# One cadence for the modulation sums, in halves of a row, and one filling quantum a group moved to the last pair

## The chip, the cores and the metric

The kernel runs on one core of one Trainium2 chip. A core has a matrix engine (TensorE, PE in the profile, its weight loads as PEld), VectorE (DVE), ScalarE (ACT), GpSimd (POOL) and SyncE (SP), which here only issues DMAs. Each engine works through its own queue of instructions in order. The metric is the device time of one execution in microseconds (us).

## The reference

One encoder block for 256 tokens of width 2048, in float32:

```python
mod = silu(c) @ W_ada + b_ada          # six parts of 2048: shift_m, scale_m, gate_m, shift_f, scale_f, gate_f
h = rms_norm(x, norm_mix_w) * (1 + scale_m) + shift_m
proj = h @ w_in                        # mLSTM q,k,v,o,i,f | GDN qkv, z, beta, a | merge gates
y_a = (sigmoid(a_o) * rms_norm(bidirectional(mlstm)(...))) @ w_branch_a
y_b = (rms_norm(bidirectional(gated_delta)(...)) * silu(b_z)) @ w_branch_b
g_a, g_b = split(sigmoid(merge), 2)
x = x + gate_m * ((g_a * y_a + g_b * y_b) @ w_out)
hf = rms_norm(x, norm_ffn_w) * (1 + scale_f) + shift_f
x = x + gate_f * ((silu(hf @ W_gate) * (hf @ W_up)) @ w_down)
out = rms_norm(x, norm_final_w)
```

The mLSTM has 4 heads. The gated delta rule (GDN) has 16 heads and runs in both directions in chunks of 64 tokens; each chunk needs the inverse of a triangular matrix. `c` is a single row, so each part of `mod` is a product of a vector with a 2048x2048 matrix.

## The kernel before, in words

**Matrix products.** Weights come from memory as float32 tiles `raw` of 1 MB (three buffers), issued on SyncE's queue (L178, L210). Each half of a tile, 128x1024, is split into a high part `wh`, rounded on ScalarE (L182, L213), and a low part `wl`, the rest, on VectorE (L184, L215). TensorE then makes three products: high by high, low by high and high by low (L187 to L189 with 128x256 results in `fjob`, L234 to L236 with 128x512 results in `tjob`). `fjob` and `tjob` are generators. One `yield` is a quantum: half a `raw` tile, its `wh`, its `wl`, and 24 matmuls of 256 columns or 12 of 512.

**Filling.** The GDN heads are chains of small dependent steps between TensorE, VectorE and ScalarE. Between two such steps the program puts quanta of projections as filler: `fill(n)` (L269) takes n quanta from the list `fills`. Where the list or a stage is run out, what is left follows later; the number of quanta in all does not depend on where they are put.

**Stages.** The first stage (to about 131 us) makes parts 0 and 1 of `mod` and the first product; then come the first heads and, from about 300 us, four groups g of four GDN heads. A group has: `gdn_blocks(g)`, which loads the inverted 32x32 blocks from memory into `cg` on POOL's queue (L723), transposes them on VectorE (L725) and mixes them into `R` (L729, L730); and two pairs of heads, `gdn_phase2`, each a chain p1 (L761), p2 (L770), p3 (L783), p4 (L795), `pa`, `pb`, `pc` (L808, L819), `po` (L829 to L834), the norm (L857 to L868), and `px` (L841), whose result `obt` goes to memory (`ob_d`, L846). Between the groups stands the inversion for the next one (`invert`), with its own fills. At a group's start the loads of `cg` are issued, then `fill(8)` runs, and then come the transpose and `R`.

After the last pair come the first mLSTM heads (`pden` L962, `ph` L978) and the projection of the GDN result, `acc_yb`: its input is read back from `ob_d` into `o4` on POOL's queue (L1076) and split into `obh` (ScalarE, L1080) and `obl` (VectorE, L1081). The mLSTM's projection `acc_ya` and the output projection `acc_o` follow. The last group of `acc_o` ends in a chain of VectorE and ScalarE steps, `tmss` (L1213), the sum with x (L1216), squares (L1217) and roots, up to the transposes `pxn` (L1336) with which the FFN begins (gate, up, down, to 1960 us). `gt0`, the first gate projection, has its first two splits made ahead.

**Modulation rows.** The rows of parts 2 to 5 of `mod` are summed beside all this. Sixteen blocks of 128 rows make a part. `ask()` loads a 128x2048 block, 1 MB, into `ada` on SyncE's queue (L116); `add()` multiplies it on VectorE by the row `silu(c)` and sums it into one column of `mod` (L124); the last block of a part adds the bias (L127). `pump()` runs once a quantum and decides: in the pairs, in y_b, and in the FFN there is one buffer (`room`), a sum is owed every `every` quanta, and it is made when the load is more than two quanta old and the pair is not in its first three steps (`held`); the load for the next follows in the quantum after. Between the groups' pairs, during the inversion, `every` is 0. From the end of the last pair (L1121) until `drive(cores, 3)` (L1146) `every` is 0. From `acc_ya` on, parts 2 to 4 have three buffers in another pool (`sr`), `every` is 4, and in `acc_o` it is 0, with sums called by name at eight quanta and the rest (`sums(P)`) at the fifth quantum of the last group. In the FFN part 5 takes one row every 8 quanta.

**Order.** A scheduler places the instructions of each engine; those wrapped in `order()` (`keep_in_program_order`) stay as written among themselves.

Of the kernel before, what the change touches and what calls it, by code (L numbers as in the profile page):

```python
# [29 lines left out]
PK_ADAB = 0  # L30
PK_NMIX = 96
PK_NFFN = 112
# [20 lines left out]
def hybrid_block(ctx: ExitStack, tc: tile.TileContext, xr, nfr, crow, pk_d, cst_d, ada2, ada4, win0, winb, wint, wba, wbb, wo, wgu, wd, out, dbg=None):  # L53
    nc = tc.nc
    V, S, G, PE = nc.vector, nc.scalar, nc.gpsimd, nc.tensor

    def pool(stack, name, bufs=1, **kw):
        return stack.enter_context(tc.tile_pool(name=name, bufs=bufs, **kw))

    cp = pool(ctx, "cp")  # L60
    st = pool(ctx, "st")
    rows_p = pool(ctx, "rows")
# [9 lines left out]
    def order(ins, yes=True):  # L72

        return tc.keep_in_program_order(ins) if yes else ins
# [5 lines left out]
    row_c = crp.tile([P, D + 2], F32, name="crow")  # L80
    pk = cp.tile([P, PK_N], F32, name="pk")
# [13 lines left out]
    mods = cp.tile([P, 2, 2, KB], F32R, name="mods")  # L95
    epsc = cp.tile([P, 1], F32, name="epsc")
    V.memset(epsc, EPS)
    mod = cp.tile([P, 96], F32, name="mod")


    V.memset(row_c[:, D:], 1.0)
# [3 lines left out]
        order(S.activation(row_c[:, g * 512 : (g + 1) * 512], pc_, AF.Silu))  # L105


    room = [(rows_p, "ada", 1, 1)]
    asked, unasked, age = [], [], [0]

    def ask():

        pl, tag, bufs, _ = room[0]
        part, b = unasked.pop(0)
        raw = pl.tile([P, D], F32, tag=tag, bufs=bufs, name=f"ada{part}_{b}")
        order(nc.sync.dma_start(raw, ada4[part - 2, b]))  # L116
        asked.append((part, b, raw))
        age[0] = 0

    def add():  # L120

        part, b, raw = asked.pop(0)
        c = part * KB + b
        order(V.scalar_tensor_tensor(raw, raw, 1.0, row_c[:, :D], ALU.mult, ALU.mult, accum_out=mod[:, c : c + 1]))  # L124
        if b == KB - 1:
            c = slice(part * KB, part * KB + KB)
            V.tensor_tensor(mod[:, c], mod[:, c], pk[:, PK_ADAB + c.start : PK_ADAB + c.stop], ALU.add)  # L127

    def ada_parts(*parts):
        unasked.extend((part, b) for part in parts for b in range(KB))  # L130

    def raw_tile(shape, name):

# [5 lines left out]
    def settle(keep=0, only=None):  # L139

        now = [f for f in behind if only is None or f.__name__ == only]
        for f in now[: len(now) - keep]:
            behind.remove(f)
            f()

    count, every = [0], [0]
    owed, held = [0], [False]

    def sums(n=1):

        while n and (unasked or asked):
            while unasked and len(asked) < room[0][3]:
# [149 lines left out]
    heads, parts = {}, {}  # L302
# [190 lines left out]
    with ExitStack() as s0:  # L493
# [35 lines left out]
        ra, raw = loads(0)  # L529
# [18 lines left out]
        for b in range(KB):  # L548
            if b:
                ra, raw = loads(b)  # L550
# [332 lines left out]
    def drive(gen, n=2):  # L883
        for _ in gen:
            fill(n)
# [140 lines left out]
    for g in range(4):  # L1026
        blocks = gdn_blocks(g)
        next(blocks)
        fill(8)
        next(blocks)  # L1030
        fill(1)
        pairs = [gdn_phase2(g, p) for p in range(2)]
        if g == 3:
            settle()
            sf.close()
            mq["pool"] = pool(sq_, "mq", side="right")
            first2 = [mlstm(h) for h in range(2)]
            for c in first2:
                next(c)
        every[0] = 1  # L1040
        for p in range(2):
            pieces = stream(4 * g + 2 * p + 4)
            for n in range(1, 10):

                held[0] = n < 4
                if p == 0:
                    next(blocks, None)
                next(pairs[p], None)
                if g == 3 and n == (8, 4)[p]:
                    next(first2[p])  # L1050
                for _ in range(last[n] if g == 3 else second[n] if p else after[n]):
                    next(pieces)
            for _ in pairs[p]:
                pass

            if g < 3:
                while 4 * g + 2 * p + 5 not in heads:
                    next(pieces)
        if g < 3:
            fills.insert(0, z_job(g + 1))  # L1060
            every[0] = owed[0] = 0
            invert(g + 1)
# [93 lines left out]
    gm = room[0][0].tile([P, D], F32, name="gm")  # L1156
    dgs = {}

    def row_diag(part, g, rp):
        ms = mods[:, part == 5]  # L1160
        if not g:
            m = mod[:, part * KB : (part + 1) * KB]
            V.tensor_copy(ms[:, 0], m)
            V.tensor_tensor(ms[:, 1], m, ms[:, 0].bitcast(F32), ALU.subtract)
        dg = dgs[part, g] = rp.tile([P, 2, 4, P], F32R, tag="dg", bufs=2, name=f"dg{part}_{g}")
        for i in range(2):
            V.tensor_tensor(
                dg[:, i], ident.unsqueeze(1).broadcast_to([P, 4, P]),
                ms[:, i, 4 * g : 4 * g + 4].bitcast(F32).unsqueeze(2).broadcast_to([P, 4, P]), ALU.mult,
            )  # L1170
# [6 lines left out]
            PE.matmul(pr, onesr, woven(dg[:, i]), start=i == 0, stop=i == 1)  # L1177
        S.activation(woven(dst[:, g * 512 : (g + 1) * 512]), pr.rearrange("p (c h) -> p c h", h=2), AF.Copy)

    every[0] = 4  # L1180
    for g in range(4):
        for i, _ in enumerate(y_a(g)):
            if g and i == 3:
                merged(g - 1, mgh, mgl)
            if i in (1, 5) and g < 2:
                row_diag(2, 2 * g + i // 4, room[0][0])
# [72 lines left out]
    affn = xp.tile([P, KB], F32, name="affn")  # L1259
# [45 lines left out]
    for g in range(4):  # L1305
        if g == 3:
            root()
        for i, _ in enumerate(o_job(g, front_o if g == 3 else None) if g else o_first, 0 if g else 2):
            if i in ((4, 7), (2, 5), (2, 5), (0, 2))[g]:
                sums()  # L1310
            if g == 3 and i == 4:
                sums(P)
                V.scalar_tensor_tensor(
                    affn, mod[:, 4 * KB : 5 * KB], 1.0, pk[:, PK_NFFN : PK_NFFN + KB], ALU.add, ALU.mult
                )
    if dbg is not None and "x1" in dbg:
        G.dma_start(dbg["x1"], x1)
    room[0] = (rows_p, "ada", 1, 1)
    ada_parts(5)
    sw.close()  # L1320
    sr_.close()
# [9 lines left out]
    def block(b):  # L1331

        px = gps(f"pxn{b}")
        for t in range(2):
            f = b % 4 * P
            order(PE.transpose(px[:, t * P : (t + 1) * P], xns[b // 4][:, t, f : f + P], ident))  # L1336
        hfs[b] = hp.tile([P, T], F32, tag="hf", bufs=2, name=f"hf{b}")
        f, m = affn[:, b : b + 1], mod[:, 3 * KB + b : 3 * KB + b + 1]
# [12 lines left out]

        return scaled, high
# [89 lines left out]
    for g in range(4):  # L1442
        c = slice(g * 512, (g + 1) * 512)
# [119 lines left out]
```

## Time and profile before

| what | us |
|---|---|
| median of 3 runs | 1972.22 |
| lowest, highest | 1970.23, 1975.39 |
| profiled execution, its own time | 1972.89 |
| its span | 1970.8 |
| mean granted TensorE clock | 0.993 of full |

The span is the time from the first to the last instruction; the profiled execution's own time is 2.1 us longer. A line of a group gives line, engine, operation, output<-input, shape and count, then busy time, mean time of one in ns, and the idle time of the engine before it. A line of the timeline gives start, duration, engine, line and operation; in brackets the idle time before it and who ended it. A line of waits gives who waited for whom: total, how many times, longest. A line of a DMA issue ends in KB and the median time from issue to landing in us.

### The profile page before, as it was taken

How to read it: one execution, taken by the hardware profiler on the slowest of the kernel's cores; microseconds unless marked ns; L12 is line 12 of the kernel's file. 1: busy time of each engine (PE TensorE's matmuls, PEld its weight loads, DVE VectorE, ACT ScalarE, POOL GpSimd, SP SyncE). 2: the span in 40 equal slices, each digit the busy share in tenths (PEclk: the TensorE clock that was granted, in tenths of full speed). 3: DMA queues.
4: the chain of work that ended last, by engine and by line, in shares of the span. 5: the costliest groups of instructions: out<-in, count | busy, mean ns of one | idle time of the engine just before them, and what ended most of it. 6: DMA issues, size and time to landing. Idle time of an engine off the chain costs nothing.

```text
span 1970.8 us, 27090 instructions
## 1 busy us (share of the span) xinstructions
PE 1929.8 (98%) x10418; PEld 1705.2 (87%) x10418; DVE 1405.4 (71%) x2067; ACT 1025.8 (52%) x1551; POOL 116.6 (6%) x211
## 2 busy tenths in 40 slices
PE   8999999999999999999999999999999999999998
PEld 6878889998999899889787888788888888888886
DVE  6779886887788788866577878866665665555554
ACT  3137646765776577565534444644444444444444
POOL 0001210111011101110100000200000000000000
PEclk9999999999999999999899999999999999999999
DMA  9987676667576766686776888576676665565553
GB/s 399 420 349 233 182 255 241 217 221 235 213 219 214 243 209 219 208 293 244 242 296 247 343 301 333 206 255 236 241 268 239 235 239 207 195 214 199 207 199 143
DMA packets 78962, 485.64 MB, mean 246 GB/s; under 512 B 10585, under 2 KB 15969, under 8 KB 24433
## 3 DMA queue, kind: packets, MB, share of 16 engines
q1 hardware_dynamic: 63216, 450.69, 62.6%
q0 software_dynamic: 8160, 17.88, 4.4%
q10 hardware_dynamic: 7458, 15.36, 2.0%
q8 instruction: 81, 1.33, 0.3%
q14 instruction: 47, 0.39, 0.1%
HBM read 467.07 MB, written 16.82 MB: 246 GB/s over the span
## 4 chain that ended last, share of the span: by engine, by line
PE 85%; DVE 6%; DMA 5%; ACT 2%; issue 1%; SPq 0%; ACTq 0%; DVEq 0%
PE acc_gt L234 4%; PE acc_gt L235 4%; PE acc_gt L236 4%; PE acc_up L234 4%; PE acc_up L235 4%; PE acc_up L236 4%; PE acc_d L234 4%; PE acc_d L236 4%; PE acc_d L235 4%; DMA ra<-ada 3%; PE acc_b L187 2%; PE acc_b L189 2%; PE acc_o L236 2%; PE acc_b L188 2%; PE acc_o L234 2%; PE acc_o L235 2%
## 5 line engine op out<-in xcount | busy, mean ns | idle before, releaser
L215 DVE TENSOR_TENSOR wl_d<-raw_d,wh_d 128x1024 fp32r<-128x1024 f32 x88 | 107.7, 1224 | 105.9 <-ACT wh_d L213 105.9
L215 DVE TENSOR_TENSOR wl_up<-raw_up,wh_up 128x1024 fp32r<-128x1024 f32 x88 | 107.6, 1224 | 100.2 <-ACT wh_up L213 100.1
L215 DVE TENSOR_TENSOR wl_gt<-raw_gt,wh_gt 128x1024 fp32r<-128x1024 f32 x88 | 108.1, 1229 | 79.4 <-ACT wh_gt L213 79.4
L187 PE MATMUL acc_b<-hh,wh_b 128*128 128x256 f32 x576 | 162.8, 283 | 0.0
L189 PE MATMUL acc_b<-hh,wl_b 128*128 128x256 f32 x576 | 159.4, 277 | 0.1
L188 PE MATMUL acc_b<-hl,wh_b 128*128 128x256 f32 x576 | 159.1, 276 | 0.0
L213 ACT ACTIVATE wh_d<-raw_d 128x1024 fp32r<-128x1024 f32 x88 | 92.9, 1056 | 126.3 <-PE acc_d L235 118.9
L213 ACT ACTIVATE wh_gt<-raw_gt 128x1024 fp32r<-128x1024 f32 x88 | 92.9, 1056 | 121.2 <-PE acc_gt L235 71.0
L213 ACT ACTIVATE wh_up<-raw_up 128x1024 fp32r<-128x1024 f32 x88 | 92.8, 1056 | 108.1 <-PE acc_up L235 77.1
L124 DVE SCALAR_TENSOR_TENSOR ada<-ada,crow 128x2048 f32<-128x2048 f32 x64 | 145.9, 2283 | 0.0
L234 PE MATMUL acc_gt<-wh_gt,hfh 128*128 128x512 f32 x352 | 135.9, 386 | 0.0
L235 PE MATMUL acc_gt<-wh_gt,hfl 128*128 128x512 f32 x352 | 135.1, 384 | 0.0
L236 PE MATMUL acc_gt<-wl_gt,hfh 128*128 128x512 f32 x352 | 134.2, 381 | 0.0
L234 PE MATMUL acc_up<-wh_up,hfh 128*128 128x512 f32 x352 | 133.4, 379 | 0.0
L235 PE MATMUL acc_up<-wh_up,hfl 128*128 128x512 f32 x352 | 133.4, 379 | 0.0
L236 PE MATMUL acc_up<-wl_up,hfh 128*128 128x512 f32 x352 | 133.4, 379 | 0.0
L234 PE MATMUL acc_d<-wh_d,ffh 128*128 128x512 f32 x344 | 130.5, 379 | 0.0
L235 PE MATMUL acc_d<-wh_d,ffl 128*128 128x512 f32 x344 | 130.5, 379 | 0.0
L236 PE MATMUL acc_d<-wl_d,ffh 128*128 128x512 f32 x344 | 130.4, 379 | 0.0
L561 PE MATMUL first<-x,raw 128*128 128x256 f32 x512 | 114.5, 382 | 7.4 <-ACT x L555 7.0
L561 PEld LDWEIGHTS first<-x,raw 128*128 128x128 f32 x512 | 96.0, 190 | 25.9 <-ACT x L555 12.6
L188 PEld LDWEIGHTS acc_b<-hl,wh_b 128*128 128x128 f32 x576 | 111.3, 193 | 0.1
(382 smaller groups left out, 5262.1 us busy)
## 6 DMA issues: line engine op xcount, KB each, us to landing
ada<-ada SPq DMA_DIRECT2D x64, 1024.0 KB, 6.2
raw_gt<-wgu SPq DMA_DIRECT2D x44, 1024.0 KB, 4.9
raw_up<-wgu SPq DMA_DIRECT2D x44, 1024.0 KB, 4.9
raw_d<-wd SPq DMA_DIRECT2D x44, 1024.0 KB, 4.9
raw_b<-winb SPq DMA_DIRECT2D x36, 1024.0 KB, 5.0
ra<-ada SPq DMA_DIRECT2D x32, 1025.0 KB, 15.6
raw<-win SPq DMA_DIRECT2D x16, 1024.0 KB, 14.5
raw_z<-wint SPq DMA_DIRECT2D x16, 1024.0 KB, 5.2
```

Of the source, the lines that this page charges most:

```text
L124: order(V.scalar_tensor_tensor(raw, raw, 1.0, row_c[:, :D], ALU.mult, ALU.mult, accum_out=mod[:, c : c + 1]))
L187: PE.matmul(o, wh[:, k], woven(hh[:, kk]), start=kk == 0, stop=False)
L188: PE.matmul(o, wh[:, k], woven(hl[:, kk]), start=False, stop=False)
L189: PE.matmul(o, wl[:, k], woven(hh[:, kk]), start=False, stop=kk == KB - 1)
L213: order(S.activation(wh, raws[u][:, k0 : k0 + 2], AF.Copy), early)
L215: order(V.tensor_tensor(wl, raws[u][:, k0 : k0 + 2], wh.bitcast(F32), ALU.subtract), early)
L234: order(PE.matmul(ps[t], xh[:, kk, c], woven(wh[:, k]), start=kk == 0, stop=False), early and steps > 1)
L235: PE.matmul(ps[t], xl[:, kk, c], woven(wh[:, k]), start=False, stop=False)
L236: PE.matmul(ps[t], xh[:, kk, c], woven(wl[:, k]), start=False, stop=kk == last)
L561: PE.matmul(first[o], raw[:, o], x[:, b], start=b == 0 and o % 2 == 0, stop=b == KB - 1 and o % 2 == 1)
```

## The change

1. Each row block is loaded and summed in two halves of 128x1024 (512 KB). The first half is summed into `mod`, the second into `later_half`; after the last half of a part, `later_half` and the bias are added. Sums and adds are all in program order. There are two buffers, always in the pool `rows_p`, and each half asked for has its own age. `mod` keeps only parts 2 to 5 (64 columns), so its indices shift by two parts.
2. `pump()` has one rule for all stages: age all that is asked, ask for one more half if fewer than two are asked, then make one sum if one is owed, the oldest is more than two quanta old, and it is not held. `every` stays 1 from the last group's pairs to the last group of `acc_o`. The three-buffer stage, the calls by name in `acc_o`, and the pause after the last pair are gone; `held` is cleared there instead. In the last group of `acc_o`, after its fourth quantum, the rest is summed and `affn` made. In the FFN `every` is 4 instead of 8.
3. At the starts of groups 1 to 3 `fill(8)` becomes `fill(7)`.

By the built programs VectorE has 2040 instructions instead of 1972 (64 sums and 4 adds more), SyncE 505 instead of 441 (64 loads more), ScalarE 1548 instead of 1546; TensorE and POOL have as many as before (9711 and 216). The three quanta of part 3 stand as 36 matmuls of `acc_ma3` between `po` and `px` of the last pair. On ScalarE the two `ev_ma3` with their table load come ahead of that pair's `obt`, and one `wh_yb` ahead of its second store of `ob_d`. At the groups' starts the transpose of `cg` comes one `wl` earlier on VectorE. In the first pair of each group the four `pa` matmuls stand as one and three, with filling matmuls between. On VectorE the last half sum, `mod` and `affn` stand among the `tmss` steps of the last group of `acc_o`.

```diff
-    mod = cp.tile([P, 96], F32, name="mod")
+    mod = cp.tile([P, 64], F32, name="mod")
...
-    room = [(rows_p, "ada", 1, 1)]
-    asked, unasked, age = [], [], [0]
+    asked, unasked = [], []
+    later_half = cp.tile([P, KB], F32, name="later_half")
     def ask():
-        pl, tag, bufs, _ = room[0]
-        part, b = unasked.pop(0)
-        raw = pl.tile([P, D], F32, tag=tag, bufs=bufs, name=f"ada{part}_{b}")
-        order(nc.sync.dma_start(raw, ada4[part - 2, b]))
-        asked.append((part, b, raw))
-        age[0] = 0
+        part, b, i = unasked.pop(0)
+        raw = rows_p.tile([P, D // 2], F32, tag="ada", bufs=2, name=f"ada{part}_{b}_{i}")
+        c = slice(i * (D // 2), (i + 1) * (D // 2))
+        order(nc.sync.dma_start(raw, ada4[part - 2, b, :, c]))
+        asked.append([part, b, i, raw, 0])
     def add():
-        part, b, raw = asked.pop(0)
+        part, b, i, raw, _ = asked.pop(0)
+        part -= 2
         c = part * KB + b
-        order(V.scalar_tensor_tensor(raw, raw, 1.0, row_c[:, :D], ALU.mult, ALU.mult, accum_out=mod[:, c : c + 1]))
-        if b == KB - 1:
+        order(V.scalar_tensor_tensor(raw, raw, 1.0, row_c[:, i * (D // 2) : (i + 1) * (D // 2)], ALU.mult, ALU.mult, accum_out=later_half[:, b : b + 1] if i else mod[:, c : c + 1]))
+        if b == KB - 1 and i:
             c = slice(part * KB, part * KB + KB)
-            V.tensor_tensor(mod[:, c], mod[:, c], pk[:, PK_ADAB + c.start : PK_ADAB + c.stop], ALU.add)
+            order(V.tensor_tensor(mod[:, c], mod[:, c], later_half, ALU.add))
+            order(V.tensor_tensor(mod[:, c], mod[:, c], pk[:, PK_ADAB + 2 * KB + c.start : PK_ADAB + 2 * KB + c.stop], ALU.add))
...
     def pump():
         count[0] += 1
-        age[0] += 1
+        for a in asked:
+            a[-1] += 1
         if every[0] and count[0] % every[0] == 0:
             owed[0] = 1
-        if room[0][3] > 1:
-            if owed[0]:
-                owed[0] = 0
-                sums()
-        elif asked:
-            if owed[0] and age[0] > 2 and not held[0]:
-                owed[0] = 0
-                add()
-        elif unasked and every[0]:
+        if unasked and every[0] and len(asked) < 2:
             ask()
+        if asked and owed[0] and asked[0][-1] > 2 and not held[0]:
+            owed[0] = 0
+            add()
...
-        fill(8)
+        fill(7 if g else 8)
...
-    every[0] = owed[0] = 0
+    held[0] = False
     cores = steps(*first2)
...
     drive(cores, 3)
-    every[0] = 1
     drive(steps(mlstm(2), mlstm(3)), 3)
...
-    if asked:
-        add()
-    room[0] = (pool(sr_, "sr"), "sr", 3, 3)
...
-    every[0] = 4
     for g in range(4):
         for i, _ in enumerate(y_a(g)):
...
-    every[0] = 0
...
-            if i in ((4, 7), (2, 5), (2, 5), (0, 2))[g]:
-                sums()
-            if g == 3 and i == 4:
+            if g == 3 and i == 3:
+                every[0] = owed[0] = 0
                 sums(P)
                 V.scalar_tensor_tensor(
...
-    every[0] = 8
+    every[0] = 4
```

More of the change, by code (lines that the diff above doesn't have):

```diff
@@ L105, in c_row @@
         order(S.activation(row_c[:, g * 512 : (g + 1) * 512], pc_, AF.Silu))
-    room = [(rows_p, "ada", 1, 1)]
-    asked, unasked, age = [], [], [0]
+    asked, unasked = [], []
+    later_half = cp.tile([P, KB], F32, name="later_half")
     def ask():
-        pl, tag, bufs, _ = room[0]
-        part, b = unasked.pop(0)
-        raw = pl.tile([P, D], F32, tag=tag, bufs=bufs, name=f"ada{part}_{b}")
-        order(nc.sync.dma_start(raw, ada4[part - 2, b]))
-        asked.append((part, b, raw))
-        age[0] = 0
+        part, b, i = unasked.pop(0)
[3 more added lines that the diff above has]
+        asked.append([part, b, i, raw, 0])
     def add():
-        part, b, raw = asked.pop(0)
+        part, b, i, raw, _ = asked.pop(0)
+        part -= 2
         c = part * KB + b
-        order(V.scalar_tensor_tensor(raw, raw, 1.0, row_c[:, :D], ALU.mult, ALU.mult, accum_out=mod[:, c : c + 1]))
-        if b == KB - 1:
+        order(V.scalar_tensor_tensor(raw, raw, 1.0, row_c[:, i * (D // 2) : (i + 1) * (D // 2)], ALU.mult, ALU.mult, accum_out=later_half[:, b : b + 1] if i else mod[:, c : c + 1]))
+        if b == KB - 1 and i:
             c = slice(part * KB, part * KB + KB)
-            V.tensor_tensor(mod[:, c], mod[:, c], pk[:, PK_ADAB + c.start : PK_ADAB + c.stop], ALU.add)
+            order(V.tensor_tensor(mod[:, c], mod[:, c], later_half, ALU.add))
+            order(V.tensor_tensor(mod[:, c], mod[:, c], pk[:, PK_ADAB + 2 * KB + c.start : PK_ADAB + 2 * KB + c.stop], ALU.add))
     def ada_parts(*parts):
-        unasked.extend((part, b) for part in parts for b in range(KB))
+        unasked.extend((part, b, i) for part in parts for b in range(KB) for i in range(2))
     def raw_tile(shape, name):
@@ L151, in sums @@
         while n and (unasked or asked):
-            while unasked and len(asked) < room[0][3]:
+            while unasked and len(asked) < 2:
                 ask()
@@ L1152, in hybrid_block @@
     sr_ = ExitStack()
-    if asked:
-        add()
-    room[0] = (pool(sr_, "sr"), "sr", 3, 3)
-    gm = room[0][0].tile([P, D], F32, name="gm")
+    sr = pool(sr_, "sr")
+    gm = sr.tile([P, D], F32, name="gm")
     dgs = {}
@@ L1161, in row_diag @@
         if not g:
-            m = mod[:, part * KB : (part + 1) * KB]
+            m = mod[:, (part - 2) * KB : (part - 1) * KB]
             V.tensor_copy(ms[:, 0], m)
@@ L1185, in hybrid_block @@
             if i in (1, 5) and g < 2:
-                row_diag(2, 2 * g + i // 4, room[0][0])
+                row_diag(2, 2 * g + i // 4, sr)
             if i in (3, 7) and g < 2:
                 row_spread(2, 2 * g + i // 4, gm)
-    every[0] = 0
     def o_job(g, front=None):
@@ L1308, in hybrid_block @@
         for i, _ in enumerate(o_job(g, front_o if g == 3 else None) if g else o_first, 0 if g else 2):
-            if i in ((4, 7), (2, 5), (2, 5), (0, 2))[g]:
-                sums()
-            if g == 3 and i == 4:
+            if g == 3 and i == 3:
+                every[0] = owed[0] = 0
                 sums(P)
                 V.scalar_tensor_tensor(
-                    affn, mod[:, 4 * KB : 5 * KB], 1.0, pk[:, PK_NFFN : PK_NFFN + KB], ALU.add, ALU.mult
+                    affn, mod[:, 2 * KB : 3 * KB], 1.0, pk[:, PK_NFFN : PK_NFFN + KB], ALU.add, ALU.mult
                 )
@@ L1317, in hybrid_block @@
         G.dma_start(dbg["x1"], x1)
-    room[0] = (rows_p, "ada", 1, 1)
     ada_parts(5)
@@ L1337, in block @@
         hfs[b] = hp.tile([P, T], F32, tag="hf", bufs=2, name=f"hf{b}")
-        f, m = affn[:, b : b + 1], mod[:, 3 * KB + b : 3 * KB + b + 1]
+        f, m = affn[:, b : b + 1], mod[:, KB + b : KB + b + 1]
         def scaled():
```

## The prediction

> **What bounds the kernel now.** I read the page's totals first, then the waits of TensorE, then short windows around each wait.
>
> ```profile
> span 1970.8 us, 27090 instructions
> PE 1929.8 (98%) x10418; PEld 1705.2 (87%) x10418; DVE 1405.4 (71%) x2067; ACT 1025.8 (52%) x1551; POOL 116.6 (6%) x211
> PEclk9999999999999999999899999999999999999999
> ```
>
> TensorE is busy 98% of the span, VectorE 71%. No matmul is added or removed here, so the change can win only TensorE's idle time or its stretches at half clock. The waits view gives for each waiting line the total, the count and the longest wait in us:
>
> ```profile
> PE acc_o L236 <- DVE wl_o L215: 3.7, 4, 2.1
> PE px L841 <- DVE on L868: 3.6, 1, 3.6
> PE pxn L1336 <- ACT xn L1272: 1.8, 1, 1.8
> PE p L795 <- DVE pt L784: 0.7, 1, 0.7
> ```
>
> The windows view has length, busy time of PE, PEld, DVE, ACT and POOL (with counts), granted clock, DMA share and GB/s:
>
> ```profile
> 952.00:955.40 3.40, 0.00 (x0) 0.00 (x1) 1.22 (x7) 2.52 (x10) 0.00 (x0) 1.00 0.33 136
> 955.40:965.70 10.30, 10.30 (x34) 7.64 (x35) 1.31 (x9) 1.76 (x5) 2.59 (x4) 0.50 0.32 107
> 965.70:973.40 7.70, 7.70 (x21) 3.39 (x19) 4.61 (x5) 4.78 (x9) 1.21 (x2) 1.00 0.92 311
> 1023.70:1027.10 3.40, 3.40 (x27) 3.27 (x27) 2.28 (x7) 0.90 (x3) 0.00 (x0) 1.00 0.90 315
> 1027.10:1030.50 3.40, 3.40 (x10) 2.68 (x9) 1.69 (x3) 0.87 (x1) 0.00 (x0) 0.50 0.87 293
> 1256.00:1960.00 704.00, 703.66 (x3292) 612.11 (x3293) 411.19 (x398) 322.02 (x353) 10.86 (x6) 1.00 0.61 218
> ```
>
> The reader should see one hole: after the last pair's output matmuls TensorE idles 3.4 us and more, then works 10.3 us at clock 0.50. The FFN (last row) has no hole: TensorE is busy 703.66 of 704.
>
> **The change, term by term.** The filling quanta first. One quantum is 12 matmuls of 128x512, starting 0.216 us apart (nine steps between the first two rows below take 1.94 us), so 2.6 us. Three are taken from the starts of groups 1 to 3; in the changed program's order they stand as 36 matmuls of `acc_ma3` between `po` and `px` of the last pair.
>
> ```profile
> 683.77 0.38 PE L236 MATMUL acc_o<-wl_o,hh 128*128 128x512 f32 x1
> 685.71 0.38 PE L236 MATMUL acc_o<-wl_o,hh 128*128 128x512 f32 x1
> 685.92 0.97 PE L761 MATMUL p<-R,cc 128*128 128x32 f32 x8
> 955.40 0.73 PE L841 MATMUL px<-cst,on 128*128 128x128 f32 x2 [3.63 <-DVE on L868]
> 958.88 0.45 PE L841 MATMUL px<-cst,on 128*128 128x128 f32 x1
> 973.36 0.78 PE L234 MATMUL acc_yb<-wh_yb,obh 128*128 128x512 f32 x1
> ```
>
> (1a) The 3.63 us before `px` get 3 x 2.6 = 7.8 us of work: −3.6. These quanta are moved, so their own time costs nothing. Each brings a `wh` on ScalarE (1.06, rows below) and a `wl` on VectorE (1.23), and every second one a 1 MB load on SyncE's queue. A `wl` that came ahead of the last `on` steps would hold `px` by 1.2 each, three of them 3.7; the spare cover is 7.8 − 3.63 = 4.2, so `px` is still not late. The loads only keep their order among the weight loads; POOL's queue, with the loads of `cg` and `o`, gets nothing new, though `cg` is now asked with one quantum less ahead of it (term 4).
>
> (1b) From `px` to the first `acc_yb` matmul pass 973.36 − 955.40 = 18.0 us, 10.3 of them at half clock. Without the idle gap the clock should be full at `px`. At full clock TensorE's own work there would take some 18.0 − 10.3/2 = 12.9 us. But `acc_yb` also waits for a round trip through memory:
>
> ```profile
> 959.37 0.84 ACT L845 ACTIVATE obt<-px,pk 128x256 f32<-128x256 f32 x2 [4.82 <-PE px L841]
> 962.63 1.51 POOL L1076 DMA_DIRECT2D o<-ob_d  x2 [55.44 <-ACT dn L964]
> 968.78 1.06 ACT L1080 ACTIVATE obh<-o 128x1024 fp32r<-128x1024 f32 x1 [0.40 <-DMA o<-ob_d]
> 969.87 1.23 DVE L1081 TENSOR_TENSOR obl<-o,obh 128x1024 fp32r<-128x1024 f32 x1 [0.24 <-ACT obh L1080]
> L355 ACT ACTIVATE ev_ma<-acc_ma 128x512 f32<-128x512 f32 x4 | 2.2, 594 | 0.0
> ```
>
> From the last `px` (958.88 + 0.45 = 959.33) to `obl` (969.87 + 1.23 = 971.10) it takes 11.8 us. New in front of it on ScalarE, by the changed order, are the two `ev_ma3` (2 x 0.594 = 1.2) ahead of `obt`, and one `wh_yb` (1.06, as the equally large `obh`) ahead of the second store of `ob_d`. With 0.5 for `px` at full clock: 0.5 + 1.2 + 1.06 + 11.8 = 14.5. And a stretch of `pden`'s tiny matmuls can itself be followed by a slow slot: the window 1023.7 to 1027.1 is full, holds 24 of them, and the next one runs at 0.50. I take 15.0, hence −3.0; ends: −5.1 (TensorE alone bounds) and 0.
>
> [...]
>
> (2) The `o` projection. Before, the last three sums stand in a row on VectorE ahead of a `wl_o`, and `acc_o` waits 2.1 us. After, they stand one half at a time between `wl` tiles, but one last half, `mod` and `affn` come inside the final residual chain.
>
> ```profile
> 1240.48 2.29 DVE L124 SCALAR_TENSOR_TENSOR ada<-ada,crow 128x2048 f32<-128x2048 f32 x1
> 1242.69 2.29 DVE L124 SCALAR_TENSOR_TENSOR ada<-ada,crow 128x2048 f32<-128x2048 f32 x1
> 1246.18 0.70 PE L236 MATMUL acc_o<-wl_o,mgh 128*128 128x512 f32 x2 [2.11 <-DVE wl_o L215]
> 1247.26 0.17 DVE L1313 SCALAR_TENSOR_TENSOR affn<-mod,pk 128x16 f32<-128x16 f32 x1
> 1249.09 1.23 DVE L215 TENSOR_TENSOR wl_gt<-raw_gt,wh_gt 128x1024 fp32r<-128x1024 f32 x1 [0.52 <-ACT wh_gt L213]
> 1250.80 0.69 DVE L1213 TENSOR_TENSOR tmss<-acc_o,gm 128x512 f32<-128x512 f32 x1 [0.22 <-PE acc_o L259]
> 1253.48 0.42 DVE L1213 TENSOR_TENSOR tmss<-acc_o,gm 128x256 f32<-128x256 f32 x1
> ```
>
> The wait of 2.1 goes. The half sum has no row; half of 2.29 is 1.15 and a `wl` of the same 128x1024 takes 1.23, so I take 1.2. From 1250.80 on VectorE is the chain that `pxn` waits for, so the half sum pushes the end by up to 1.2, and one small operation (0.17, as `affn`) by 0.2: −2.1 + 1.2 + 0.2 = −0.7; ends −2.1 (all fits in the gap before `wl_gt`) and +2.
>
> (3) Pairs. Sums sit in VectorE's queue between the steps of the chains. The nearest row is this one, a sum right ahead of `pt`, for which `p` at L795 waits 0.7:
>
> ```profile
> 697.19 2.28 DVE L124 SCALAR_TENSOR_TENSOR ada<-ada,crow 128x2048 f32<-128x2048 f32 x1
> 699.80 0.68 DVE L784 TENSOR_TENSOR pt<-p,cst 128x512 f32<-128x512 f32 x1
> L124 DVE SCALAR_TENSOR_TENSOR ada<-ada,crow 128x2048 f32<-128x2048 f32 x64 | 145.9, 2283 | 0.0
> ```
>
> A half keeps a chain waiting 1.1 us less: −0.7 there and about as much once more elsewhere, −1.5. Ends: −4 (as much in four places) and +4 (three or four new collisions of 1.2, since halves come twice as often). The 64 extra sums cost 64 x (2 x 1.2 − 2.28) = 8 us of VectorE, with the accumulator reads some more; it stands at 71%, and the FFN at 411 of 704, so I cost them at nothing; in the pairs, where that cover is thin, they are inside the +4. That sums now go on through the end of the pairs (`held` cleared instead of `every` 0) and every fourth quantum in the FFN adds no work elsewhere, for the number of rows is the same.
>
> (4) `fill(7)`. The group's start loses a quantum of cover between the loading of the inverse and `p1`:
>
> ```profile
> 678.71 0.71 DVE L725 STREAM_TRANSPOSE cg<-cg 128x512 f32<-128x512 f32 x1 [0.84 <-DMA cg<-inv_d]
> 681.49 0.48 DVE L730 SCALAR_TENSOR_TENSOR R<-cg,cst,R 128x256 f32<-128x256 f32 x1
> ```
>
> `R` is ready at 681.97 and `p1` runs at 685.92, a slack of 3.9; less 2.6 leaves 1.3, so `p1` does not wait. But VectorE waits for `cg` (0.84 already), and by the changed order the transpose stands one `wl` earlier, so the `wl` behind it comes late by about 0.5 at two of the groups: +1.0; ends 0 and 3 x 2.6 = +8.
>
> (5) The loads. 64 loads of 1 MB become 128 of 512 KB. SyncE issues 64 more; each row's first half is asked when a buffer comes free.
>
> ```profile
> ada<-ada SPq DMA_DIRECT2D x64, 1024.0 KB, 6.2
> raw_yb<-wbb SPq DMA_DIRECT2D x16, 1024.0 KB, 5.4
> gtb<-mb_d SPq DMA_DIRECT2D x4, 512.0 KB, 5.5
> SPq L116 <- DVE ada L124: 178.6, 56, 8.5
> ```
>
> A 512 KB load lands in 5.5 us, a 1 MB load in 5.4, from issue. A half is summed at least three quanta (7.8 us) after it was asked, so the loads are covered: 0. The queue is rival B.
>
> **Sum**: −3.6 − 3.0 − 0.7 − 1.5 + 1.0 = −7.8. The profiled execution took 1972.89, 0.67 above the median of the runs (1972.22); 1972.89 − 7.8 = 1965.1, and on the median 1964.4.
>
> **Rivals.** 0.3% of 1972.2 is 5.9 us, about what a measurement here can tell from no change: faster is below 1966.3, slower above 1978.1.
>
> A: the gap is only shifted. The quanta cover the 3.63, but `acc_yb` then waits for the round trip, the clock falls there (term 1b is 0 or lost again), and `cg` eats a few us: −3.6 + 0 − 0.7 + 0 + 2 = −2.3, 1969.9 on the median. For it: 14.5 of round trip against 12.9 of TensorE work. Against: TensorE's idle there would be 2 us, under the 3.4 that stood before the slow stretch. Chance 0.22.
>
> B, slower: the SyncE queue. Weights and rows share it, and an ask whose buffer is still being summed stands at its head with the weight loads behind it: 56 such waits, 178.6 us, 3.2 each. With two asks a row there are about twice as many, and from the `y_a` stage on two half buffers replace three whole ones. It decides where the wait exceeds what `raw` tiles are early by. If one in eight of the 96 halves before the FFN made TensorE wait a half sum (1.2): 12 x 1.2 = +14.4; −7.8 + 14.4 = +6.6, 1978.8. For it: the 8.5 us longest wait. Against: each wait is for a half as long a sum, and TensorE now shows no wait for a weight load. Chance 0.20. [...]
>
> C: the quanta do their work and the clock stays full, TensorE alone bounding (1b −5.1, 3 −4): −3.6 − 5.1 − 0.7 − 4 + 1 = −12.4, 1959.8. It belongs to the forecast's side.
>
> **How the numbers follow.** Forecast 0.45, C 0.13, A 0.22, B 0.20. Faster: all of the forecast but a tenth that ends beyond its bound, and C: 0.41 + 0.13 = 0.54. Same: A, that 0.04 and 0.01 of B: 0.27. Slower: 0.19. The range takes in A and C and goes up to where two thirds of B are left out: 1957 to 1977. The forecast's own range, with its terms' nearer ends, is 1959 to 1969.
>
> **What would show it.** Right: no wait over 0.5 us at `px` L841; the last pair's half-clock stretch 3.4 us or less; `px` to the first `acc_yb` in 14 to 16 us; no 2.1 us wait of `acc_o` on `wl_o`; `pxn` waiting about 1.2 longer; L124 128 times at about 1.2. Wrong: new TensorE waits of over 1 us behind `cg`, `R` or `wl` at the starts of groups 1 to 3, half-clock slots there, or ScalarE's `wh` waiting on `raw` loads that before it did not.

## The result, and the profile after

The changed kernel took 1976.78 us at the median of 22 runs, the kernel before 1973.45 in its 22 runs: a ratio of 1.0014, 95% interval 1.0008 to 1.0020, so 1.6 to 3.9 us slower. The forecast was 1964.4, faster. The profiled execution's span is 1973.7 us, 2.9 above that of before. A trace shows one execution, and executions of one program differ: e6's trace below is of the fastest of its 11 runs, 3.9 us under their median, e4's is of one 2.8 us above.

The same views of the kernel after: the page's head, then the waits of TensorE and one of SyncE's queue (line numbers are lower by 3 to 10).

```profile
span 1973.7 us, 27332 instructions
PE 1929.3 (98%) x10418; PEld 1704.7 (86%) x10418; DVE 1412.1 (72%) x2199; ACT 1029.5 (52%) x1553; POOL 116.5 (6%) x211
```

```profile
PE ph L975 <- ACT dn L961: 4.6, 1, 4.6
PE pa L805 <- DVE UL L741: 3.5, 3, 1.2
PE pxa L991 <- DVE hal L996: 3.4, 1, 3.4
PE pxn L1326 <- ACT xn L1264: 2.5, 1, 2.5
PE acc_o L233 <- DVE wl_o L212: 1.4, 2, 1.0
SPq L116 <- DVE ada L124: 240.2, 118, 7.9
```

The wait of `px` is gone, as intended, and the 2.1 us wait of `acc_o` is down to at most 1.0. Three waits are new: `ph` on `dn` (4.6), `pa` on `UL` (three times 1.2; 0.2 in all before), `pxa` on `hal` (3.4). The next fence is the timeline of TensorE after the last pair, the one behind it ScalarE's and ScalarE's DMA queue (ACTq), then a line of SyncE's queue and the window after the idle time of `ph`.

```profile
956.12 0.60 PE L838 MATMUL px<-cst,on 128*128 128x128 f32 x4
956.56 2.74 PE L959 MATMUL pden<-ones,mdec 128*128 128x1 f32 x24
966.56 10.16 PE L975 MATMUL ph<-vt,mdec 128*128 128x512 f32 x18 [4.58 <-ACT dn L961]
976.15 0.78 PE L231 MATMUL acc_yb<-wh_yb,obh 128*128 128x512 f32 x1
1004.07 0.44 PE L991 MATMUL pxa<-cst,hs 128*128 128x128 f32 x2 [3.45 <-DVE hal L996]
```

```profile
957.06 0.33 ACTq L353 DMA_DIRECT2D ma_d<-ev_ma  x1
957.48 0.39 ACTq L843 DMA_DIRECT2D ob_d<-obt  x1
966.33 0.24 ACT L961 ACTIVATE dn<-pden 128x4 f32<-128x4 f32 x2 [6.99 <-DMA ob_d<-obt]
1001.10 1.06 ACT L210 ACTIVATE wh_yb<-raw_yb 128x1024 fp32r<-128x1024 f32 x1 [4.92 <-DMA raw_yb<-wbb]
```

```profile
954.46 0.33 SPq L116 DMA_DIRECT2D ada<-ada  x1
```

```profile
964.10:970.90 6.80, 4.34 (x5) 1.85 (x6) 1.34 (x7) 2.22 (x6) 2.59 (x4) 0.50 0.62 217
```

`px` runs at full clock without a wait (1.00 from 956.1 to 958.8; four in 0.60 us, 0.73 for two before), yet `acc_yb` starts 20.0 us later (18.0 before). `dn` stands on ScalarE behind the store of `ob_d`, and that store is late; a half row was asked 1.7 us ahead of `px`, at 954.46. TensorE idles 4.58 and falls to half clock again (0.50 in the window). Then the weights of y_b are late: `wh_yb` waits 4.92 for its load, `hah` and `hal` stand behind it, and `pxa` waits. The last view is the windows of both kernels over the start of y_b, before first (columns as in the prediction), and from the DMA view of the 66 us around it, before's and after's landing times of these stores and loads.

```profile
967.00:1003.00 36.00, 36.00 (x160) 28.39 (x159) 26.54 (x34) 22.50 (x35) 6.77 (x11) 1.00 0.85 302
ob_d<-obt ACTq DMA_DIRECT2D x2, 128.0 KB, 1.7
raw_yb<-wbb SPq DMA_DIRECT2D x7, 1024.0 KB, 6.0
```

```profile
967.00:1003.00 36.00, 33.30 (x130) 24.08 (x129) 25.25 (x33) 19.72 (x30) 9.18 (x15) 0.95 0.95 339
ob_d<-obt ACTq DMA_DIRECT2D x2, 128.0 KB, 8.3
raw_yb<-wbb SPq DMA_DIRECT2D x7, 1024.0 KB, 8.4
ada<-ada SPq DMA_DIRECT2D x6, 512.0 KB, 5.9
```

The DMA engines are busy 95% of that stretch instead of 85%, the stores of `ob_d` land 6.6 us later after their issue, the weights 2.4 us. The last figure alone does not mark the loss: by the same view the weights take 8.5 us in e1 and 8.3 in e8, told below, which lose less. Where the time went, by start times of the same matmuls in the traces of all kernels (e1 and so on as numbered below). `move` says whether the three quanta were moved; `rows` how rows are loaded between the last pair and the end of the first mLSTM heads (`thin` is e6's 8 columns); `px` is the first of the last pair; the last three columns are the time from `px` to the first `acc_yb` and to the first `acc_ya`, and the landing time of `ob_d`; all in us.

```
        move  rows       px  acc_yb  acc_ya     pxn  acc_up  px-yb  px-ya  ob_d
before  no    none    955.4   973.4  1078.7  1255.0  1283.8   18.0  123.3   1.7
after   yes   halves  956.1   976.2  1085.5  1259.2  1286.8   20.0  129.4   8.3
e1      yes   none    952.3   967.7  1076.2  1255.1  1283.9   15.4  123.9   5.7
e2      no    halves  957.7   975.5  1081.6  1260.1  1287.3   17.8  123.9   1.8
e3      yes   none    954.5   971.7  1077.7  1257.2  1293.0   17.2  123.3   5.7
e4      yes   whole   953.1   968.5  1082.9  1256.3  1284.5   15.3  129.8   5.7
e5      yes   halves  954.1   974.6  1083.7  1258.0  1285.3   20.5  129.7   8.4
e6      yes   thin    953.9   971.2  1077.7  1252.1  1279.4   17.3  123.8   6.1
e7      yes   whole   953.6   968.5  1078.9  1252.8  1280.3   14.9  125.3   5.1
e8      yes   none    951.9   968.0  1076.1  1248.9  1277.2   16.1  124.2   5.2
e9      yes   none    955.4   970.8  1076.7  1254.1  1283.4   15.4  121.3   5.1
e10     no    none    957.9   975.9  1081.3  1254.2  1283.0   18.0  123.4   1.7
e11     yes   none    951.7   969.2  1076.8  1249.7  1278.3   17.5  125.1   6.1
```

After against before: +0.7 at the last `px` (which needs no 3.6 us wait any more), +2.8 at `acc_yb`, +6.8 at `acc_ya`, then back to +3.0 by the end of `acc_o` and the FFN's head. The programs of after, e3, e5, e6 and e9 hardly differ up to the last `px`, and yet it starts between 953.9 and 956.1; so a difference of 2 us between two traces says little.

### The profile page after: what moved, and what is told of

The parts are those of the page before. It is cut to its first block, busy times and chain, and to the rows that moved or that the text cites. A ratio compares the mean times of both kernels' runs of the same rounds, so it can differ in the third digit from the quotient of the medians.

```text
span 1973.7 us, 27332 instructions
## 1 busy us (share of the span) xinstructions
PE 1929.3 (98%) x10418; PEld 1704.7 (86%) x10418; DVE 1412.1 (72%) x2199; ACT 1029.5 (52%) x1553; POOL 116.5 (6%) x211
## 5 line engine op out<-in xcount | busy, mean ns | idle before, releaser
L124 DVE SCALAR_TENSOR_TENSOR ada<-ada,crow 128x1024 f32<-128x1024 f32 x128 | 155.9, 1218 | 7.0 <-DMA ada<-ada 7.0
L184 PEld LDWEIGHTS acc_b<-hh,wh_b 128*128 128x128 f32 x576 | 111.9, 194 | 0.1
```

Of the source, the lines that this page charges most:

```text
L124: order(V.scalar_tensor_tensor(raw, raw, 1.0, row_c[:, i * (D // 2) : (i + 1) * (D // 2)], ALU.mult, ALU.mult, accum_out=later_half[:, b : ...
L184: PE.matmul(o, wh[:, k], woven(hh[:, kk]), start=kk == 0, stop=False)
```

## The experiments

Three theories were put up. 1: the moved quanta put the 512 KB store `ma_d` right ahead of `ob_d` in ScalarE's DMA queue, and this makes `ob_d` late; its rival: the DMA engines are full, whichever queue. 2: the rows that are now loaded from the last pair into y_b take the place of y_b's weights. 3: the halves change the order of `pa` and `UL` on the engines. Rival to 2 and 3: halving costs by the number of loads and sums.

**e1, the move alone** (on the kernel before)

```diff
-        fill(8)
+        fill(7 if g else 8)
```

> The kernel before with only fill(7) at the starts of groups 1 to 3. Theory 1 (the moved quanta make ev_ma3 end right before px, so its 512 KB store ma_d stands in ScalarE's DMA queue just ahead of the two ob_d stores, and dn and the loads of o wait for them): no wait at px, ob_d lands in 6 us or more from issue (1.7 before), ph waits 3 to 5 us for dn, a half-clock stretch of 6.8 follows; time within 2 us of the kernel before. Rival 1 (the store is late because the half loads now go on after the last pair): no sums run in this stretch here, so ob_d lands in under 3 us, ph does not wait, the half-clock stretch goes, and the time is 5 to 7 us under the kernel before.

Median 1972.3, ratio 0.9994 (0.9985 to 1.0003). The stretch did what the prediction said: no wait at `px`, 15.4 us from `px` to `acc_yb`, 5.7 us won there. `ob_d` landed in 5.7 us, between what the two theories said, and `ph` waited 0.4 us:

```profile
960.25 7.99 PE L978 MATMUL ph<-vt,mdec 128*128 128x512 f32 x18 [0.42 <-ACT dn L964]
```

But the 5.7 won are gone by `pxn`. Of them 3.1 go in y_b, between `acc_yb` and `acc_ya`, though the rows are paused at its start. Then `acc_ya` waits 3.2 in two places, the longer one behind three sums in a row that the old scheme makes at the head of `acc_ya`, so the move alone also shifts when sums fall due:

```profile
PE acc_ya L236 <- DVE wl_ya L215: 3.2, 2, 2.2
```

**e2, the change without the move**: `fill(8)` throughout in the changed kernel.

> The changed kernel with fill(8) again at every group's start. Theory 1: ma_d is stored well ahead of px, ob_d lands in about 2 us, px waits 3.6 us again and the half-clock stretch of some 10 us is back; px to the first acc_yb about 18 us. The wait of pxa (3.5 us) in y_b and the split pa with its 1.2 us waits stay, so the time is 4 to 8 us over the kernel before. Rival 1: ob_d lands in 6 us or more here too, and px to acc_yb takes over 20 us.

1976.3, ratio 1.0021 (1.0009 to 1.0033). `px` waits 3.6 again, `ob_d` lands in 1.8, both as theory 1 said. The wait of `pxa`, though, is only 0.8, with the same row loads, and `acc_ya` comes 123.9 us after `px`, as before (123.3). y_b starts no later than in the changed kernel (975.5 against 976.2), but the last load of its weights ahead of it is asked at 950.1 instead of 955.9; whether that is the reason no run shows. So the row loads delay y_b only together with the move. What costs here is the end of `acc_o`, where one more half is left to sum and `pxn` waits 6.2.

**e3, the sums paused** from the end of the last pair, as before

```diff
-    held[0] = False
+    every[0] = owed[0] = 0
...
     drive(cores, 3)
+    every[0] = 1
```

> The changed kernel with the sums paused from the end of the last pair to the end of the first mLSTM heads, as before. Theory 2 (rows loaded in this stretch delay the weights of y_b): the 3.5 us wait of pxa and the half-clock slot behind it go, about 4 us faster than the changed kernel, some 1973. Theory 1: ob_d still lands in 6 us or more and ph still waits over 3 us for dn. Rival 1: ob_d lands in under 3 us, that wait goes too, and the time is about 1968.

1981.8, ratio 1.0042 (1.0029 to 1.0054), against the 1973 expected. The stretch itself did as theory 2 said: `pxa` waits 0.7, `acc_ya` starts 7.8 us earlier than in the changed kernel, at 1077.7 (1.6 of them stand at `px` already, where the pause has not begun), and `ob_d` lands in 5.7, so the row loads had a part in that too. But nine halves, instead of the changed kernel's four, are left to sum at the end, and the edit so makes a new stall there:

```profile
PE acc_gt L231 <- ACT hfh L1341: 7.9, 1, 7.9
PE pxn L1327 <- ACT xn L1265: 7.0, 1, 7.0
```

Its total therefore says nothing of theory 2; e8 and e9 repeat it without the late sums.

**e4, whole rows** in the changed kernel's cadence

```diff
-        raw = rows_p.tile([P, D // 2], F32, tag="ada", bufs=2, name=f"ada{part}_{b}_{i}")
+        raw = rows_p.tile([P, D], F32, tag="ada", bufs=1, name=f"ada{part}_{b}")
...
-        if unasked and every[0] and len(asked) < 2:
+        if unasked and every[0] and len(asked) < 1:
```

> The changed kernel with whole rows (1 MB, one buffer, one sum for four quanta, the same cadence, the sums going on after the last pair). Theory 3 (the halves let the scheduler split the four pa matmuls of each group's first pair, so that pa waits 1.2 us for UL): the three waits go, 3 to 4 us less by the last pair. Theory 2: pxa in y_b still waits 3 us or more, for the bytes loaded there are the same; together 1973 to 1974. Rival 2 (all losses come from halving, by the larger number of loads on SyncE's queue): both waits go, 1969 or less.

1970.66, ratio 0.9986 (0.9977 to 0.9995). The three waits of `pa` are gone and the last `px` comes 3.0 us earlier than after: theory 3 holds for the waits. `pxa` still waits, 2.3 where theory 2 asked for 3 or more, and `acc_yb` itself another 3.6 on `wl_yb`, so `acc_ya` is at 1082.9, 129.8 after `px`. The bytes being the same, this speaks for theory 2 against its rival; the time lies between what the two said (1973 to 1974, and 1969 or less).

One thing more changes here. The whole row is asked 5.9 us ahead of `px`, the changed kernel's half row 1.7 ahead; `ob_d` lands in 5.7 instead of 8.3, and `acc_yb` starts 15.3 after `px` instead of 20.0:

```profile
947.24 0.33 SPq L114 DMA_DIRECT2D ada<-ada  x1
ob_d<-obt ACTq DMA_DIRECT2D x2, 128.0 KB, 5.7
```

e5 and e7, below, repeat the pair (8.4 and 20.5 with halves, 5.1 and 14.9 with whole rows). No run moved that load by itself.

**e5, the store on another queue**: in the changed kernel

```diff
-            S.dma_start(dst, ev)
+            (G if name == "ma3" else S).dma_start(dst, ev)
```

> The changed kernel with the last ma_d store issued on POOL's queue instead of ScalarE's; everything else stands in the same order. Theory 1 (the 512 KB ma_d store ahead of the ob_d stores in one queue makes these land late): ob_d lands in 2 to 4 us from issue instead of 8.3, the 4.6 us wait of ph on dn goes or is under 1 us, the first acc_yb comes 3 to 5 us earlier after px. Rival 1 (the DMA engines are full, whichever queue): ob_d still lands in 6 us or more and nothing moves. For the end: if the loads of the y_b stretch are its bound, the wait of pxa grows by what is won before, and the time stays within 2 us of the changed kernel.

1976.78, ratio 1.0018 (1.0008 to 1.0027), and theory 1 falls as the main cause:

```profile
ma_d<-ev_ma POOLq DMA_DIRECT2D x1, 512.0 KB, 9.2
ob_d<-obt ACTq DMA_DIRECT2D x2, 128.0 KB, 8.4
```

Alone in its queue, `ob_d` lands no earlier.

**e6, thin loads**: the six halves asked for, in program order, between the last pair and the end of the first mLSTM heads bring 8 columns each.

```diff
+        if thin[0]:
+            few = rows_p.tile([P, 8], F32, tag="few", bufs=2, name=f"few{part}_{b}_{i}")
+            order(nc.sync.dma_start(few, ada4[part - 2, b, :, c.start : c.start + 8]))
```

> The changed kernel, but the six halves that are loaded between the last pair and the end of the first mLSTM heads bring 8 columns each instead of 1024 (the sums there multiply those columns over and over, so these six sums leave most of the rows out); the number of loads and sums and the order on every engine are the same. Theory 2 as bandwidth (3 MB of rows more in a stretch in which the DMA engines are full): the 3.5 us wait of pxa and the half-clock slot after it go, about 4 us faster, and ob_d lands in 5 to 6 us like in the paused kernel, 2 us more. Rival 3 (the place in the queues counts: one more entry for each half on SyncE, and a sum on VectorE that waits for its load with wl_yb behind it): pxa still waits 2 us or more and the time is within 2 us of the changed kernel.

1972.22, ratio 0.9990 (0.9982 to 0.9999), 4.6 us under the changed kernel at the medians; this kernel leaves most of six half rows out of its sums. `acc_ya` starts at 1077.7, as in e3, `raw_yb` lands in 6.0 and `ob_d` in 6.1. `pxa` still waits 2.3, which theory 2 had not expected: part of the wait for y_b's weights is there without the 3 MB. The number of loads and sums is that of the changed kernel, but not their order on SyncE's queue: with buffers of their own, the first two thin loads are asked from 937.43 on, ahead of two weight loads, where the changed kernel asks at 949.14 and 954.46, behind them. The other four stand in the same places, in y_b; from `acc_yb` to `acc_ya` it takes 106.5 us instead of 109.4. So there the bytes cost; for the landing of `ob_d` the run does not part the bytes from the place.

**e7, whole rows and the store on POOL**

> The kernel with whole rows (the fourth experiment) and the last ma_d store on POOL's queue. Theory 1: the wait of ph on dn (2.0 us there) goes and ob_d lands in 2 to 4 us; the first acc_yb comes 2 us earlier. Theory 2: the weights of y_b, and not the start, bound that stretch, so the gain is gone by the first acc_ya, and the time is that of the fourth experiment, 1970 to 1971. If the start bounds it, 1968 to 1969.

1969.49, ratio 0.9984 (0.9975 to 0.9993), by the intervals no different from e4; `acc_yb` starts at 968.5 in both, so the start is hardly won earlier by the store's queue, though the wait of `ph` on `dn` is gone. `acc_ya` comes 125.3 us after `px`, with the row loads of e4, where it was 129.8; the medians differ by 1.2 only, so one of these traces, e4's by its place among its runs, overstates the loss in y_b.

**e8, whole rows, paused, caught up later**: e7 with the pause of e3; from `acc_ya` on two buffers and one row every three quanta.

```diff
+    room[0] = (sr, "sr", 2)
+    every[0] = 3
```

> The kernel with whole rows and the last ma_d store on POOL's queue, and the rows paused from the last pair to the end of the first mLSTM heads; from acc_ya on two buffers and one row every three quanta, so that no row is left for the end of acc_o. Theory 2: no wait of pxa over 1.5 us, no half-clock slot after it, the first acc_ya 4 us or more ahead of the fourth experiment's, and, with no late sums, 1965 to 1967, under both kernels. Rival 3 (what is gained at y_b is lost again to sums made faster in acc_ya and acc_o, as the 2 us wait of acc_o on wl_o showed before): 1969 to 1972.

1966.49, ratio 0.9956 (0.9944 to 0.9969), the first version clearly under both kernels (by at least 6 us to the kernel before, by its interval). No row is left for the end, and `acc_ya` starts 6.9 us earlier than in e4, but only 2.8 earlier than in e7, from which it differs by the pause and the catching up.

**e9, the same with halves**, the extra ones called for by name in `acc_ya` and `acc_o` (fourteen such calls stand in the kernel, not the ten of the expectation)

> The eighth experiment's scheme with halves instead of whole rows: the changed kernel with the last ma_d store on POOL's queue, the sums paused from the last pair to the end of the first mLSTM heads, and ten more halves summed in acc_ya and acc_o so that at most one is left for the end. Theory 3 (halves cost what the split pa shows and little else): the three waits of pa on UL (1.2 us each) are there, the last px comes 2.5 to 3.5 us later than in the eighth experiment, and the time is 1969 to 1970. Rival 2 (halving costs more, by twice the loads and sums in every stage): 1972 or more. If the halves are harmless: 1966 to 1967.

1969.92, ratio 0.9983 (0.9971 to 0.9995), within the expected 1969 to 1970, with the waits of `pa` back and the last `px` 3.5 later than in e8:

```profile
PE pa L805 <- DVE UL L741: 3.5, 3, 1.2
```

That the time was met is luck in part. By `acc_ya` e9 is only 0.6 behind e8; the rest is lost from there to `pxn`, which takes 177.4 us instead of 172.8, where the rows are caught up by another scheme. So e9 against e8 is not the price of the `pa` waits.

**e10, e8 without the move**

> The eighth experiment with fill(8) at every group's start, so without the move of three quanta. The prediction's working for the move alone (3.6 of idle, 3.0 of half clock, 1.0 lost behind cg: 5.6 together) says: px waits 3.6 us again, a half-clock stretch of some 10 us follows, px to the first acc_yb takes 18 us, and the time is 1971.5 to 1973. If the loads of the y_b stretch bound it whenever it starts, the first acc_ya is no later than in the eighth experiment and the time is 1966 to 1968.

1969.89, ratio 0.9981 (0.9972 to 0.9990), less than the 1971.5 expected: 3.4 us over e8 at the medians, 5.8 in the profiled spans (1970.0 against 1964.2). The ratios give 4.9. The move is worth about that where nothing takes it back; the prediction's steps gave 5.6 for it. `px` waits 3.6 again, and `acc_yb` starts 18.0 after it.

**e11, e8 with the store back on ScalarE**

> The eighth experiment with the last ma_d store back on ScalarE's queue. By the fifth experiment (ob_d landed no earlier with ma_d on another queue) the queue does not matter: ob_d lands in 5 to 6.5 us and the time is 1965 to 1968. If the store's place in the queue matters once no row loads are about: ob_d lands 1 us or more later than in the eighth experiment, and the time is 1968 to 1969.

1965.89, ratio 0.9960 (0.9947 to 0.9972): for the time the queue does not matter here either. In the stretch itself it does a little where no half row stands ahead of the store: with `ma_d` on POOL `ob_d` lands 0.6, 0.6 and 0.9 us earlier (e7 against e4, e9 against e3, e8 against e11), the wait of `ph` on `dn` of 2.0, 2.2 and 2.5 us is gone but for 0.3 in e8, and `acc_yb` comes 0.5, 1.8 and 1.4 us sooner after `px`. Theory 1 names a small part of the delay, then. This version, which needs nothing but whole rows and the pause, as before, the move, and the new asking and catching up, is as good as e8.

By these ratios, each against the kernel before (1973.4 x ratio): the new asking and catching up with whole rows, −3.7 (e10); the move, −4.9 more (e8); halves, caught up by name, +5.3 (e9); sums that go on after the last pair, +6.1 (the change itself). They add up to +2.8. Each step has an uncertainty of about 3 us. Other pairs give the last two again: halves +5.5 (the change against e4) and +6.7 (e5 against e7); sums that go on, +5.5 (e7 against e8) and +5.1 (e4 against e11). Halves and sums that go on are not independent: only both together, with the move, bring the 20 us from `px` to `acc_yb`.

## Why the prediction was wrong, point by point

That 1976.78 lies inside the stated range, at its upper end, is no merit of the working: the forecast was a gain of 7.8 us, and a loss of 1.6 to 3.9 was measured.

**(1a), the wait of `px`: right.** It is gone after and in e1. **(4), `fill(7)`: not contradicted.** In e1 the last `px` comes 3.1 earlier where the 3.63 alone would give that much, so about 0.5 was lost on the way, against +1.0; by one trace each that is within the noise, but it is far from the end of +8.

**(1b), −3.0 with ends −5.1 and 0: this step failed.** Measured +2.1 (20.03 instead of 17.96 us). For the move alone it held: e1, with nothing else changed, gave 15.4 where 15.0 was forecast, and the other runs with the move and no rows there (e3, e8, e9, e11) 15.4 to 17.5. In part that was luck. The working took the round trip of 11.8 us over from a trace in which `ob_d` landed in 1.7 and the DMA engines were busy 0.32 of the time up to 965.7 (the quoted window from 955.4). In e1 weights flow in those microseconds (the DMA engines are busy 0.80 of the time from 957 to 967), `ob_d` lands in 5.7, and `obl` is ready 16.5 us after `px` instead of the 14.5 worked out; but the first matmuls of `acc_yb` take `obh` and need not wait for it. What the step left out is the row loads, which it put at nothing. With a half row asked 1.7 us ahead of `px`, `ob_d` lands in 8.3 (8.4 in e5), `ph` waits 4.6, and `acc_yb` starts after 20.0 us (20.5). So 0 was no end of the range. That the clock would be full for lack of an idle gap failed with it, since the 4.6 us wait made a new one, with 0.50 from 964.1 to 970.9. The slow slot that the step feared behind `pden` came in e1 and e8 (there the six `ph` behind them take 4.52 us, 2.82 after; below).

**"Sums go on through the end of the pairs … adds no work elsewhere", costed at nothing, and (5), the loads at 0: these failed most.** The number of rows is the same, but not the stretch they are loaded in. By the ratios it costs 5.1 to 6.1 us that the sums go on. The e3 and e6 timelines put `acc_ya` 7.8 us earlier than after, at 1077.7 in both; 1.6 and 2.2 of that stand at the last `px` already, which leaves 6.2 and 5.6. A part is the late start of `acc_yb` (1b), the rest is lost in y_b, where the weights come late. The error was to look at landing times from issue, one load at a time, and not at the DMA share, which stood in the quoted windows (0.92 from 965.7, 0.90 at 1023.7) and which no step used. The share alone does not decide, though: e2 has the same row loads and 0.96 from 967 to 1003, and loses nothing up to `acc_ya`. Why the loads cost there only with the move stays open.

**(3), pairs, −1.5: wrong sign, within its ends.** The last `px` comes 3.0 and 3.5 us later with halves in two pairs of traces (e4 against after, e8 against e9), and 2.2 later in the mean of the five kernels with halves and the move (954.8) against the four with whole rows (e4, e7, e8, e11: 952.6). No sum stood in front of a chain; halves changed the scheduler's order so that one `pa` runs ahead and three wait 1.2 us in each of three groups for `UL`:

```profile
342.01 1.17 DVE L741 COPY UL<-cg 32x256 f32<-32x256 f32 x4
343.24 0.49 PE L805 MATMUL pa<-vv,UL 128*128 128x128 f32 x2 [1.16 <-DVE UL L741]
```

The split of `pa` stood in the changed order and was seen, as the change's description shows; the prediction gave it no price. The 5.5 to 6.7 us that halves cost in all are more than these waits; the rest falls, in the traces of e5 and e7, between `px` and `acc_yb`.

**(2), the `o` projection, −0.7: right in sign, too small.** From the first `acc_ya` to `pxn` 2.6 us are won, 3.8 to `acc_up`, more than the end of −2.1, and `acc_ya` with its new cadence is in that. The half sum inside the last chain cost 0.7 there (`pxn` waits 2.5 instead of 1.8), not 1.2.

**Rival B** named the right side and nearly the right place for the bound (weights late behind rows), by the wrong mechanism: the asks on SyncE's queue wait longer, 240.2 us in 118 waits, yet the weights were late behind transfers under way, not behind waiting asks. That is the likelier reading, not a shown one: in e6, 4.6 us faster, the asks from 925 to 1006 wait less for their buffers too, 10.3 us instead of 17.4. **Rival A**, a gap only shifted, is nearest to what happened at `ph`: the round trip does take the place of `px`'s wait, but by more than was won.

## What to carry to other kernels

Filling TensorE's idle gap here also took away the quiet time of what stood behind it (`ob_d` landed in 1.7 us before and in 5.7 in e1, by the move alone): before costing the chain that is to run there, look at which loads are asked just ahead of it and at the DMA share of the stretch, and price each store and load of that chain as in a busy stretch. Here the work that was to be spread evenly was better left out where the transfers were already the next bound, and caught up where they were not (e8, e11), but not at the end of a chain: five more late halves cost more (e3) than the pause had won. Two edits can each be harmless in a stretch and cost there together (`px` to `acc_ya`: 123.9 in e1 and in e2, 129.4 after), so each is worth a run with and without the other. A different size of a side task can change a scheduler's order far from it, and the new order should be priced line by line.

## What the runs showed of the hardware

The two stores of `ob_d`, 128 KB each, landed later where more was under way: in 1.7 or 1.8 us in a quiet stretch (before, e2, e10; DMA share before 0.23 from 958.8 to 962.2), in 5.1 to 6.1 in eight runs with a 1 MB weight load asked 0.2 us ahead of `px`, in 8.3 with a half row asked 1.7 us ahead of it as well (after; DMA share 0.92 from 958.8 to 962.2), and in 8.4 in that case with `ma_d` on another queue (e5).

TensorE's clock fell in two places without an idle gap just before. In e8 the 4 us before are busy throughout (4.00 of 4.00), with `pden`'s tiny matmuls at their end, and the next 3.5 us run at 0.51:

```profile
951.40:955.40 4.00, 4.00 (x33) 3.68 (x32) 0.52 (x2) 3.18 (x6) 0.54 (x1) 1.00 0.70 213
955.40:958.90 3.50, 3.50 (x6) 1.35 (x4) 0.97 (x1) 0.00 (x0) 0.00 (x0) 0.51 0.72 281
```

Before has the same at 1027.1: a window busy 3.40 of 3.40, with 128x1 matmuls in it, and 0.50 in the next 3.4 us (of its 24 small matmuls 21 start in the window from 1023.7; the prediction counted all). In the changed kernel the same 24, from 956.56 on, are followed by full clock (1.00 from 958.8 to 962.2). That these matmuls are the cause was not tried by itself.
